# The compression's weight parts in one matmul of 512 columns, and its input chunk turned by VectorE and DMA

## The chip, the cores and the metric

The kernel runs on one core of a Trainium2 chip. The metric is the device time of one execution in microseconds; a run of the program is compared with runs of the other version on the same chip. Engine names are those of the profile: PE is TensorE (PEld its weight loads), DVE is VectorE, ACT is ScalarE, POOL is GpSimd, SP is the engine that issues most DMAs.

## What is computed

One layer of a hybrid decoder block on a sequence of 256 tokens and a width of 2048, in fp32. What matters for this change, cut from the reference:

```python
hn = rms_norm(h, ln_gain[l])
z = split_columns(hn @ w_in[l] + b_in[l])
y_a = rglru_branch(z['lru_x'], ...) * silu(z['lru_gate'])
k_c = rms_norm(compress(z['nsa_k_cmp'], cmp_pos[l, 0], cmp_w1[l, 0], cmp_w2[l, 0]), ...)
v_c = compress(z['nsa_v_cmp'], cmp_pos[l, 1], cmp_w1[l, 1], cmp_w2[l, 1])
y_b = nsa_branch(q_b, k_c, v_c, ...) * silu(z['nsa_gate'])
...
merged = mg[0] * (y_a @ w_branch[0]) + mg[1] * (y_b @ w_branch[1]) + mg[2] * (y_c @ w_branch[2])
h = h + merged @ w_out[l]
...
def compress(t, pos, w1, w2):        # blocks of 32 tokens, one each 16 tokens: 15 of them
    flat = blocks + pos               # 15 x 4096 for each of two heads
    return silu(flat @ w1) @ w2       # w1: 4096 x 256
```

The input projection `hn @ w_in` and the products behind it are almost all the arithmetic. The compression `flat @ w1` is a product with only 30 rows (15 blocks, two heads) for the keys and 30 for the values.

## The kernel before, in words

**The weight stream.** PE works through one long list of weight pieces, called halves (lines 76 to 155 make the list). A half is 128 partitions by 1024 columns, 512 KB, and arrives by one DMA into a `raw` tile, of which there are six. Each half is cut in two parts by `cut` (line 418): `wh`, the rounded copy that ACT makes, and `wl`, the rest, which DVE makes by subtracting `wh` from `raw`. Both kinds of tile have four buffers (line 422), so the conversion of a half may start only when PE is through with the half four places before. `by_rows` (line 440) then multiplies with three matmuls of 512 columns each, high by `wh`, high by `wl`, low by `wh`, for two k tiles and two row tiles: 12 matmuls a half, into the banks named `main`.

**Side work.** Everything else (turning results, the recurrence, attention, softmax) is written as small tasks whose steps are put between the matmuls of the stream. `Side.tick` (line 257) runs a task's next step when a clock of estimated costs, kept while the program is written out, allows it. A step that needs another engine's result calls `settle` and is held until the clock of PE stands a margin beyond the estimated end of that result; a step behind a DMA calls `landed`. So an added or removed instruction moves the place of all side work behind it, until the work catches up. Once written out, the order on each engine is fixed, and each engine works strictly in it.

**The compression.** The chunk of columns that feeds it (both `nsa_k_cmp` and `nsa_v_cmp`, 512 columns by 256 tokens) is turned by `turn_cmp` (line 719): ACT copies two PSUM banks of 128x512 to tiles `z`, PE transposes eight blocks of 128x128 into two PSUM banks, and ACT copies these with the bias into `k_zc`, four copies of 128x256. Then DVE lays the 15 overlapping blocks out as `k_xf` (128x960, once for keys, once for values), and a split gives `k_xs`: 60 columns for each of 32 positions, 30 of the high part and 30 of the low. 16 of the halves hold `w1`. For such a half the main loop (lines 1338 to 1350) runs, for four k tiles, a matmul of 256 columns with `wh` and another with `wl`, both with the same 60 columns of `k_xs` as the weights that stay in the array, and into one bank (`cmpb`), keys in its left 256 columns and values in its right. `cmp_end` (line 829) copies the whole bank to `hs`, 60x512, and goes on from there.

**What else stands near.** `turn_chunk` (line 704) turns the other chunks without PE: ACT copies both banks to a `k_zt` tile, DVE transposes it in 32x32 blocks (one instruction, 128x1024), four DMAs of 128 KB on SP's queue move the blocks to their place, and ACT applies the bias. `lru_task` (line 741), one for each fourth of the recurrence, convolves on DVE (`k_uc`), splits the result into `k_ucs`, splits its gate weights into `k_wds`, and has eight matmuls of 256 columns with them. `kk_task` (line 902) normalises the attention keys: squares and scales on ACT, POOL and DVE (`k_zn`), a transpose, four DMAs that move the blocks, and copies into `kk` on ACT. `y_split` (line 1091) multiplies a branch's result with its gate and splits it into `k_yh` and `k_yl` in four parts, one for each half of the product with `w_branch`.

Of the kernel before, what the change touches and what calls it, by code (L numbers as in the profile page):

```python
# [11 lines left out]
R32 = mybir.dt.float32r  # L12
AF = mybir.ActivationFunctionType
OP = mybir.AluOpType
AX = mybir.AxisListType

P = 128
D = 2048
S = 256
NT = S // P  # L20
# [6 lines left out]
NCMP = 15  # L27
NR = 32
HID = 256
# [296 lines left out]
def block_kernel(ctx: ExitStack, tc: tile.TileContext, io):  # L326
# [6 lines left out]
    wp = pool("wp")  # L333
# [11 lines left out]
    def nm(s):  # L345
        uid[0] += 1
        return f"{s}_{uid[0]}"
# [7 lines left out]
    def two(shape, dt=F32, name="b2"):  # L355
        return k2.tile(shape, dt, tag="k2", name=nm("k2_" + name))
# [12 lines left out]
    side = Side(range(4), MOST, clock, ROOMS)  # L369
# [48 lines left out]
    def cut(h, k=0, nk=None, late=False):  # L418
        m, n = h["nk"] * h["n"], h["n"]
        nk = nk or h["nk"]  # L420
        if k == 0:
            h["whl"] = [wp.tile([P, 1024], R32, tag=x, bufs=AHEAD + 1, name=nm(x)) for x in ("wh", "wl")]
        wh, wl = h["whl"]
        for a, b in parts_of(h, k, nk):
            if late:
                A.activation(wh[:, a:b], h["raw"][:, a:b], AF.Copy)
                due.append((wl[:, a:b], h["raw"][:, a:b], f(wh[:, a:b])))
            else:
                split(wh[:, a:b], wl[:, a:b], h["raw"][:, a:b])
        h["wh"] = wh[:, :m].rearrange("p (k n) -> p k n", n=h["n"])  # L430
        h["wl"] = wl[:, :m].rearrange("p (k n) -> p k n", n=h["n"])
# [48 lines left out]
    st = {}  # L480
# [181 lines left out]
    def blocks(x):  # L662

        return x.rearrange("p (n a j) -> p n a j", a=4, j=32)
# [39 lines left out]
    def turn_chunk(read, out, into, dst, k0, name):  # L704

        yield from side.wait("rs")
        yield from side.room(k4=1)
        x = mid([P, 4 * S], name="zt")
        for t, z in enumerate(celled(x)):
            A.activation(z, cells(out[t]), AF.Copy, scale=rsr[:, t:t + 1])  # L710
        side.done.add(read)
        yield from cross(x, x, flat(dst[:, k0:k0 + 4, :]).rearrange("p (b n j) -> p b n j", b=4, j=32))
        yield from side.wait("vec")
        for q in range(0, 4, 2):
            into(dst, k0 + q, moved(x)[:, 2 * q:2 * q + 4], name)
            yield True
        side.give(k4=1)

    def turn_cmp(read, out, into, dst, k0, name):

        yield from side.wait("rs")
        z = [two([P, 512], name="z") for _ in range(NT)]
        for t in range(NT):
            A.activation(z[t], out[t], AF.Copy, scale=rsr[:, t:t + 1])
            yield True
        side.done.add(read)
        yield from side.settle()
        yield from side.wait("vec")
        for q in range(2):
            b, = yield from side.take()  # L730
            for c in range(2):
                for t in range(NT):
                    T.transpose(banks[b][:, c * S + t * P:c * S + (t + 1) * P],
                                z[t][:, (2 * q + c) * P:(2 * q + c + 1) * P], ident)
            yield True
            into(dst, k0 + 2 * q, blocks(banks[b]), name)
            side.back(b)
            yield True


    def lru_task(i):
        yield from side.wait("vec", f"lru_x{i // 2}")
# [67 lines left out]
    def cmp_task(out):  # L810

        z = mid([P, 4, S], name="zc")
        yield from turn_cmp("cmpz", out, biased_cols, z, 0, "cmp")
        st["xs"] = []
        for kv in range(2):
            x = mid([P, NR, 2 * NCMP], name="xf")
            src = z[:, 2 * kv:2 * kv + 2, :]
            win = bass.AP(tensor=src.tensor, offset=src.offset,
                          ap=[list(src.ap[0]), [1, NR], [S, 2], [16, NCMP]])
            pos = vec[:, VEC["pos"] + NR * kv:VEC["pos"] + NR * (kv + 1)]  # L820
            V.tensor_tensor(x.rearrange("p r (g i) -> p r g i", g=2), win,
                            pos[:, :, None, None].to_broadcast([P, NR, 2, NCMP]), op=OP.add)
            yield True
            xs = big([P, NR, 4 * NCMP], R32, name="xs")
            split(xs[:, :, :2 * NCMP], xs[:, :, 2 * NCMP:], x)
            st["xs"].append(xs)
            yield True

    def cmp_end():
        b = st["cmpb"]  # L830
        w2 = two([P, 2, 2, P], name="w2")
        G.dma_start(w2, io["w2"])
        hs = two([4 * NCMP, 512], name="hs")
        A.activation(hs, banks[b][:4 * NCMP, :], AF.Copy)
        yield from side.settle()

        for q in range(4):
            T.transpose(banks[b][:, q * 4 * NCMP:(q + 1) * 4 * NCMP], hs[:, q * P:(q + 1) * P],
                        ident[:4 * NCMP, :4 * NCMP])
        yield True  # L840
        hz = banks[b][:, :4 * 4 * NCMP].rearrange("p (q s i) -> p q s i", q=4, s=2)
        hp, hid, sg = (one([P, 4, 30], name="hid") for _ in range(3))
        A.activation(hp, hz[:, :, 0], AF.Copy)
        V.tensor_tensor(hp, hz[:, :, 1], hp, op=OP.add)
        A.activation(sg, hp, AF.Tanh, scale=0.5)
        V.tensor_scalar(sg, sg, 1.0, 0.5, op0=OP.add, op1=OP.mult)
        V.tensor_tensor(hid, hp, sg, op=OP.mult)

        hid2 = one([P, 2, 2, 2, 16], name="hid2")
        G.memset(hid2, 0.0)  # L850
        for i in range(2):
            V.tensor_copy(hid2[:, :, :, i, :NCMP], hid[:, 2:, :].rearrange("p q (g i) -> p q g i", g=2))
        yield from side.settle()
        for q in range(2):
            T.matmul(banks[b][:30, 128:256], hid[:, q, :], w2[:, 0, q, :], start=q == 0, stop=q == 1)
        for q in range(2):
            T.matmul(banks[b][:64, 256:256 + P], hid2[:, q].rearrange("p g c i -> p (g c i)"), w2[:, 1, q, :],
                     start=q == 0, stop=q == 1)
        yield True
        for g in range(2):  # L860
            v = banks[b][32 * g:32 * g + 32, 256:256 + P]
            for i in (g, 2 + g):
                A.activation(vc4[32 * i:32 * i + 32, g, :], v, AF.Copy)
            for i in (1 - g, 3 - g):
                V.tensor_tensor(vc4[32 * i:32 * i + 32, g, :], v, f(vc4[32 * g:32 * g + 32, g, :]), op=OP.subtract)
        yield True
        ss, kc = sml([P, 1], name="kcs"), one([P, P], name="kc")
        A.activation(kc[:30, :], banks[b][:30, 128:256], AF.Square, accum_out=ss[:30, :])
        rsqrt(ss[:30, :], ss[:30, :], HD)
        yield from side.powers()  # L870
        V.tensor_scalar(kc[:30, :], banks[b][:30, 128:256], ss[:30, :], None, op0=OP.mult)
        yield from side.settle()
        T.transpose(banks[b][:, :30], kc[:30, :], ident[:30, :30])
        yield True
        src = banks[b][:, :30].rearrange("p (g i) -> p g i", g=2)
        yield from side.wait("kk")
        split(st["kh"][:, :, 256:256 + NCMP], st["kl"][:, :, 256:256 + NCMP], src, gqn)
        side.back(b)
        yield True
# [419 lines left out]
    for i, h in enumerate(halves):  # L1299
# [28 lines left out]
        if kind == "ple":  # L1328
            out = by_rows(h, lambda k: (pTh[:, k, :], pTl[:, k, :]))
        elif kind in ("rows", "turned"):  # L1330
            out = by_rows(h, halves_of(hn))
        elif kind == "proj":
            out = by_rows(h, lambda k: (st["ys"][0][:, k, :], st["ys"][1][:, k, :]))
        elif kind == "out":
            out = by_rows(h, halves_of(st["mt"]))
        elif kind == "gate":
            out = by_rows(h, halves_of(st["ht"]))
        else:
            kv = h["key"]
            if h["first"] and kv == 0:  # L1340
                st["cmpb"] = side.free.pop(0)[0]
            for k in range(h["nk"]):
                if 2 * k == h["nk"]:
                    low_parts()
                for q, w in enumerate((h["wh"], h["wl"])):
                    T.matmul(banks[st["cmpb"]][:4 * NCMP, kv * HID:(kv + 1) * HID], st["xs"][kv][:, h["k"] + k, :],
                             w[:, k, :], start=h["first"] and k == 0 and q == 0 and kv == 0,
                             stop=h["last"] and k == h["nk"] - 1 and q == 1 and kv == 1)
            if h["last"] and kv == 1:
                side.urge("cmpend", cmp_end())  # L1350
        if h["last"]:
# [117 lines left out]
```

## Time and profile before

| | us |
|---|---|
| median of three runs (lowest, highest) | 1061.61 (1061.18, 1062.3) |
| the profiled execution, its own time | 1063.0 |
| its span, first to last instruction | 1061.2 |
| PE busy in the span | 1053.4 (99%) |
| DVE busy | 768.1 (72%) |
| ACT busy | 620.7 (58%) |

Where a row of the profile begins with two numbers they are the start and the length in us, from the start of the span. A bracket behind it is the idle time of that engine just before, with what ended it. In rows that group instructions the numbers behind the bar are the busy time of all and the mean of one in ns. All instructions are recorded by one helper, so all have the line L208; they are told apart by their tiles. Matmuls overlap, so what one costs is read from the distance between starts, not from its length.

### The profile page before, as it was taken

Reading aid. Unit: us, or ns where it says so; the run is one execution under the profiler, and the core shown is the slowest. Engines: PE = TensorE matmul, PEld = TensorE weight load, DVE = VectorE, ACT = ScalarE, POOL = GpSimd, SP = SyncE. Lnnn points to the kernel's source line nnn. Section 1 sums busy time; section 2 is a strip of 40 time slices with the busy share of each in tenths; the row PEclk is TensorE's granted clock in tenths of the full one; section 3 lists DMA queues with packets and bytes.
Section 4 is the critical chain, followed back from the end, with each engine's and each line's share of the span. In section 5 each row is a group of like instructions: output and inputs, shape, how many; then the busy total and the mean of one; then the engine's idle time right before and its main releaser. Section 6 shows DMA issues by size and latency. Waiting matters only on the chain.

```text
span 1061.2 us, 14096 instructions
## 1 busy us (share of the span) xinstructions
PE 1053.4 (99%) x4927; PEld 880.5 (83%) x4927; DVE 768.1 (72%) x1135; ACT 620.7 (58%) x940; POOL 51.3 (5%) x77
## 2 busy tenths in 40 slices
PE   9999999999999999999999999999999999999998
PEld 7888898888888888888888888888888888888886
DVE  6777888897796877668878865565766566666664
ACT  7668976867767757445646544455555444444442
POOL 0000000110000000010110000000001000000000
PEclk9999999999999999999999999999999999999999
DMA  9767867787666666568677566776676876788761
GB/s 335 262 200 250 262 204 254 241 268 228 199 211 208 188 198 206 173 225 249 196 225 237 192 222 202 225 213 213 217 242 199 262 240 217 237 250 254 280 210 60
DMA packets 86295, 237.52 MB, mean 224 GB/s; under 512 B 14024, under 2 KB 31312, under 8 KB 86224
## 3 DMA queue, kind: packets, MB, share of 16 engines
q1 hardware_dynamic: 81504, 220.87, 64.6%
q0 software_dynamic: 4720, 15.76, 5.5%
q8 instruction: 38, 0.62, 0.2%
q14 instruction: 33, 0.27, 0.1%
HBM read 215.61 MB, written 4.20 MB: 207 GB/s over the span
## 4 chain that ended last, share of the span: by engine, by line
PE 97%; DMA 1%; DVE 1%; ACT 0%; SPq 0%; issue 0%; ACTq 0%; DVEq 0%
PE main L208 92%; PE bank L208 5%; DMA k_zn<-k_zt 1%; DVE wl L208 0%; DMA raw<-in_w 0%; SPq L208 0%; ACT wh L208 0%; DVE k_zn L208 0%; DVE k_fin L208 0%; ACT kk L208 0%; DVE k_ucs L208 0%; DVE sp_nss L208 0%; ACT k_fin L208 0%; ACTq L208 0%; DVEq L208 0%
## 5 line engine op out<-in xcount | busy, mean ns | idle before, releaser
L208 ACT ACTIVATE wh<-raw 128x1024 fp32r<-128x1024 f32 (+2 forms) x388 | 401.5, 1042 | 326.8 <-PE main L208 288.6
L208 DVE TENSOR_TENSOR wl<-raw,wh 128x1024 fp32r<-128x1024 f32 (+2 forms) x388 | 460.1, 1197 | 182.2 <-ACT wh L208 181.7
L208 PE MATMUL main<-wh,k_hnh 128*128 128x512 f32 (+2 forms) x1026 | 394.7, 385 | 1.2 <-ACT wh L208 1.2
L208 PE MATMUL main<-wl,k_hnh 128*128 128x512 f32 (+2 forms) x1026 | 392.7, 383 | 1.0 <-DVE wl L208 1.0
L208 PE MATMUL main<-wh,k_hnl 128*128 128x512 f32 (+1 forms) x1024 | 392.2, 383 | 0.0
L208 PEld LDWEIGHTS main<-wh,k_hnh 128*128 128x128 f32 x1026 | 192.9, 188 | 38.6 <-ACT wh L208 2.3
L208 PEld LDWEIGHTS main<-wl,k_hnh 128*128 128x128 f32 x1026 | 192.9, 188 | 37.3 <-DVE wl L208 1.6
L208 PEld LDWEIGHTS main<-wh,k_hnl 128*128 128x128 f32 x1024 | 192.1, 188 | 37.7
L208 PE MATMUL main<-wh,k_yh 128*128 128x512 f32 x192 | 75.0, 391 | 0.0
L208 PE MATMUL main<-wh,k_yl 128*128 128x512 f32 x192 | 74.8, 389 | 0.0
L208 PE MATMUL main<-wl,k_yh 128*128 128x512 f32 x192 | 74.8, 389 | 0.0
L208 PE MATMUL main<-wh,k_mth 128*128 128x512 f32 x128 | 49.8, 389 | 0.0
L208 PE MATMUL main<-wl,k_mth 128*128 128x512 f32 x128 | 49.8, 389 | 0.0
L208 PE MATMUL main<-wh,k_mtl 128*128 128x512 f32 x128 | 49.8, 389 | 0.0
L208 PE MATMUL main<-wh,k_hth 128*128 128x512 f32 x128 | 49.8, 389 | 0.0
L208 PE MATMUL main<-wl,k_hth 128*128 128x512 f32 x128 | 49.8, 389 | 0.0
L208 PE MATMUL main<-wh,k_htl 128*128 128x512 f32 x128 | 49.8, 389 | 0.0
L208 PEld LDWEIGHTS main<-wh,k_yl 128*128 128x128 f32 x192 | 36.0, 188 | 7.5
L208 PEld LDWEIGHTS main<-wh,k_yh 128*128 128x128 f32 x192 | 36.1, 188 | 7.4
L208 PEld LDWEIGHTS main<-wl,k_yh 128*128 128x128 f32 x192 | 36.1, 188 | 7.2
L208 ACT ACTIVATE k_mg<-k_mg 128x512 f32<-128x512 f32 x24 | 15.2, 634 | 28.5 <-DVE k_mg L208 28.3
L208 PEld LDWEIGHTS main<-wh,k_mth 128*128 128x128 f32 x128 | 24.0, 188 | 5.0
(243 smaller groups left out, 952.7 us busy)
## 6 DMA issues: line engine op xcount, KB each, us to landing
raw<-in_w SPq DMA_DIRECT2D x369, 512.0 KB, 4.5
bias<-in_b_in POOLq DMA_DIRECT2D x21, 256.0 KB, 5.2
raw<-in_w SPq DMA_DIRECT2D x8, 408.0 KB, 3.8
k_pz<-k_prob SPq DMA_DIRECT2D x16, 128.0 KB, 4.3
e_dram<-k_e POOLq DMA_DIRECT2D x4, 512.0 KB, 3.6
k_merged<-k_zt SPq DMA_DIRECT2D x16, 128.0 KB, 3.3
k_xc<-in_x POOLq DMA_DIRECT2D x4, 512.0 KB, 6.3
k_hx<-k_zt SPq DMA_DIRECT2D x16, 128.0 KB, 3.7
```

Of the source, the lines that this page charges most:

```text
L208: r = call(out, *args, **kw)
```

## The change

The compression's two matmuls for a k tile become one of 512 columns: `wh` and `wl` are now the two halves of one tile `whl` (same four buffers), and the moving operand takes 256 columns of each. The bank then holds the products with `wh` and `wl` side by side, for the keys alone or the values alone. When the keys are through, ACT copies the left part to `hs`, DVE adds the right part, and the values start in the bank anew; the same is done when they are through, so the copy in `cmp_end` goes. `turn_cmp` goes too, and the chunk is turned by `turn_chunk`.

```diff
-            h["whl"] = [wp.tile([P, 1024], R32, tag=x, bufs=AHEAD + 1, name=nm(x)) for x in ("wh", "wl")]
-        wh, wl = h["whl"]
+            h["whl"] = wp.tile([P, 2, 1024], R32, tag="whl", bufs=AHEAD + 1, name=nm("whl"))
+        wh, wl = h["whl"][:, 0], h["whl"][:, 1]
...
-    def turn_cmp(read, out, into, dst, k0, name):
-        z = [two([P, 512], name="z") for _ in range(NT)]
-        for t in range(NT):
-            A.activation(z[t], out[t], AF.Copy, scale=rsr[:, t:t + 1])
-            yield True
...
-                    T.transpose(banks[b][:, c * S + t * P:c * S + (t + 1) * P],
-                                z[t][:, (2 * q + c) * P:(2 * q + c + 1) * P], ident)
-            yield True
-            into(dst, k0 + 2 * q, blocks(banks[b]), name)
...
-        yield from turn_cmp("cmpz", out, biased_cols, z, 0, "cmp")
+        yield from turn_chunk("cmpz", out, biased_cols, z, 0, "cmp")
...
-        hs = two([4 * NCMP, 512], name="hs")
-        A.activation(hs, banks[b][:4 * NCMP, :], AF.Copy)
+        hs = st["hs"]
...
                 st["cmpb"] = side.free.pop(0)[0]
+                st["hs"] = two([4 * NCMP, 512], name="hs")
+            hz = banks[st["cmpb"]][:4 * NCMP, :].rearrange("p (s n) -> p s n", s=2)
             for k in range(h["nk"]):
                 if 2 * k == h["nk"]:
                     low_parts()
-                for q, w in enumerate((h["wh"], h["wl"])):
-                    T.matmul(banks[st["cmpb"]][:4 * NCMP, kv * HID:(kv + 1) * HID], st["xs"][kv][:, h["k"] + k, :],
-                             w[:, k, :], start=h["first"] and k == 0 and q == 0 and kv == 0,
-                             stop=h["last"] and k == h["nk"] - 1 and q == 1 and kv == 1)
+                T.matmul(hz, st["xs"][kv][:, h["k"] + k, :], h["whl"][:, :, k * HID:(k + 1) * HID],
+                         start=h["first"] and k == 0, stop=h["last"] and k == h["nk"] - 1)
+            if h["last"]:
+                part = st["hs"][:, kv * HID:(kv + 1) * HID]
+                A.activation(part, hz[:, 0], AF.Copy)
+                V.tensor_tensor(part, part, hz[:, 1], op=OP.add)
```

The side work moves with it. The first place is PE just behind the first `w1` half. `bank<-…,k_xs` are the compression's matmuls, those with `k_ucs` and `k_wds` the first fourth of the recurrence. In the program before, the halves there are `wh_743` (the first one of `w1`), `wh_765` and `wh_787`, and the recurrence stands in the middle of the last of them:

```order
L208 MATMUL main_83<-wh_787,k_hnh_128 128x512
L208 MATMUL main_83<-wl_788,k_hnh_128 128x512
L208 MATMUL main_83<-wh_787,k_hnl_129 128x512
L208 MATMUL bank_87<-k_ucs_711,k_wds_811 128x256 x4
L208 MATMUL bank_88<-k_ucs_712,k_wds_811 128x256 x4
L208 MATMUL main_84<-wh_787,k_hnh_128 128x512
```

After, `whl_717` is the first half of `w1`:

```order
L208 MATMUL main_84<-whl_696,k_hnl_129 128x512
L208 MATMUL bank_88<-whl_717,k_xs_650 60x512 x4
L208 MATMUL bank_89<-k_ucs_662,k_wds_751 128x256 x4
L208 MATMUL bank_90<-k_ucs_663,k_wds_751 128x256 x4
L208 MATMUL main_83<-whl_742,k_hnh_128 128x512 x2
```

The eight matmuls of the recurrence have moved one and a half halves (18 matmuls of the stream) towards the start, right behind the first `w1` half, and all of the stream stands behind them.


The second place is DVE on the way there, up to the split of the gate weights (`k_wds`, whose low part these rows make). Before:

```order
L208 TENSOR_TENSOR wl_744<-raw_647,wh_743 128x1024
L208 STREAM_TRANSPOSE k_u_566<-k_zt_759 128x1024
L208 TENSOR_TENSOR wl_766<-raw_674,wh_765 128x1024
L208 TENSOR_TENSOR k_ucs_711<-k_uc_710,k_ucs_711 64x256 x2
L208 TENSOR_TENSOR wl_788<-raw_692,wh_787 128x1024
L208 TENSOR_TENSOR k_ucs_712<-k_uc_710,k_ucs_712 64x256 x2
L208 TENSOR_TENSOR k_wds_811<-k_wd_713,k_wds_811 128x512
```

And after, where the subtractions of the weights are `whl<-raw,whl`:

```order
L208 TENSOR_TENSOR whl_696<-raw_595,whl_696 128x1024
L208 TENSOR_TENSOR k_ucs_662<-k_uc_661,k_ucs_662 64x256 x2
L208 TENSOR_TENSOR whl_717<-raw_614,whl_717 128x1024
L208 TENSOR_TENSOR k_ucs_663<-k_uc_661,k_ucs_663 64x256 x2
L208 STREAM_TRANSPOSE k_u_547<-k_zt_736 128x1024
L208 TENSOR_TENSOR whl_742<-raw_637,whl_742 128x1024
L208 TENSOR_TENSOR k_wds_751<-k_wd_664,k_wds_751 128x512
```

The split of the gate weights stood two subtractions behind that of the first `w1` half (`wl_744`); it stands one behind it (`whl_717`) now.

The third place is DVE ahead of the product of the recurrence with `w_branch`, where the parts of `k_yl` are made (two instructions a part) and `k_mg` is the merge gate's chunk, read from PE's `main` banks. Before, with the last part:

```order
L208 STREAM_TRANSPOSE k_gn_2562<-k_zt_2792 128x1024
L208 TENSOR_TENSOR wl_2784<-raw_2682,wh_2783 128x1024
L208 TENSOR_TENSOR k_yl_567<-k_yl_567,k_gl_980 128x512
L208 TENSOR_TENSOR k_yl_2702<-k_yl_567,k_yh_2701 128x512
L208 TENSOR_TENSOR wl_2806<-raw_2721,wh_2805 128x1024
```

After, with the third and the fourth part:

```order
L208 SCALAR_TENSOR_TENSOR k_mg_2779<-main_85,rsr,bias_2646 128x512
L208 SCALAR_TENSOR_TENSOR k_mg_2780<-main_86,rsr,bias_2646 128x512
L208 TENSOR_TENSOR whl_2787<-raw_2695,whl_2787 128x1024
L208 TENSOR_TENSOR whl_2804<-raw_2712,whl_2804 128x1024
L208 TENSOR_TENSOR k_yl_548<-k_yl_548,k_gl_936 128x512
L208 TENSOR_TENSOR k_yl_2681<-k_yl_548,k_yh_2680 128x512
L208 TENSOR_TENSOR k_yl_548<-k_yl_548,k_gl_936 128x512
L208 TENSOR_TENSOR k_yl_2681<-k_yl_548,k_yh_2680 128x512
```

The third and fourth part stand behind the merge chunk now; before, all four stand ahead of it. On ACT the copy that makes the third part's `k_yh` stands behind the conversion of the half `whl_2821`, which takes the buffer of the second of the four halves of that product.

More of the change, by code (lines that the diff above doesn't have):

```diff
@@ L717, in turn_chunk @@
         side.give(k4=1)
-    def turn_cmp(read, out, into, dst, k0, name):
-        yield from side.wait("rs")
-        z = [two([P, 512], name="z") for _ in range(NT)]
-        for t in range(NT):
-            A.activation(z[t], out[t], AF.Copy, scale=rsr[:, t:t + 1])
-            yield True
[L726 to L732, printed above, removed]
-                    T.transpose(banks[b][:, c * S + t * P:c * S + (t + 1) * P],
-                                z[t][:, (2 * q + c) * P:(2 * q + c + 1) * P], ident)
-            yield True
-            into(dst, k0 + 2 * q, blocks(banks[b]), name)
-            side.back(b)
-            yield True
     def lru_task(i):
```

## The prediction

> **What bounds the kernel now.** I read the page first (busy shares, the clock, the chain that ended last), then the waits of PE, then the chain's pieces in order of time.
>
> ```profile
> PE 1053.4 (99%) x4927; PEld 880.5 (83%) x4927; DVE 768.1 (72%) x1135; ACT 620.7 (58%) x940; POOL 51.3 (5%) x77
> PEclk9999999999999999999999999999999999999999
> PE 97%; DMA 1%; DVE 1%; ACT 0%; SPq 0%; issue 0%; ACTq 0%; DVEq 0%
> PE main L208 <- ACT wh L208: 1.2, 2, 0.8
> PE main L208 <- DVE wl L208: 1.0, 2, 0.8
> ```
>
> PE is the bound: 99% busy, 97% of the chain, at one clock throughout, and its waits (us in total, times, longest) come to 2.2 us. So a change can gain little beyond the PE time it removes and those 2.2 us, and it can lose wherever it makes PE wait, since no slack on PE would take that up. What PE pays for an instruction is read from the chain (start, length, count):
>
> ```profile
> 52.32 2.75 PE main L208 x12
> 55.07 0.44 PE bank L208 x4
> 55.51 23.17 PE main L208 x102
> 78.68 0.93 PE bank L208 x8
> 155.03 0.83 PE bank L208 x7
> ...
> 159.20 0.42 DVE k_ucs L208
> ...
> 159.65 0.42 DVE k_ucs L208
> ...
> 168.69 7.62 DMA k_zn<-k_zt
> ...
> 296.06 0.73 PE bank L208 x6
> 618.34 438.03 PE main L208 x1932
> ```
>
> A matmul of 512 columns costs 438.03 / 1932 = 0.2267 us, a half of twelve 2.73 (2.75 in the first row), a group of four transposes 0.44, and the eight matmuls of 256 columns of one `w1` half 0.93, or 0.117 each. The chain leaves PE for long only once, at 155.86, through ACT, DVE (a pair of `k_ucs` among it) and the moves of `k_zn` to the copies into `kk`. There PE lost its 2.2 us:
>
> ```profile
> 177.57 0.28 PE L208 MATMUL bank<-wl,k_xs 128*60 128x256 f32 x1
> 178.70 0.51 PE L208 MATMUL main<-wh,k_hnh 128*128 128x512 f32 x1 [0.84 <-ACT wh L208]
> 179.96 0.50 PE L208 MATMUL main<-wl,k_hnh 128*128 128x512 f32 x1 [0.75 <-DVE wl L208]
> 176.41 1.28 ACT L208 ACTIVATE kk<-k_zn,gqn 128x128 fp32r<-128x128 f32 x4 [3.36 <-DMA k_zn<-k_zt]
> ```
>
> ACT stood 3.36 us for the moves, and the next half's conversion stood behind it. Without a wait the two matmuls of `main` would have started at about 177.7 and 177.9; the second started at 179.96.
>
> **The change, term by term, on PE.** *Transposes.* Two groups of four go: −2 × 0.44 = **−0.88 us**, at 52 and 55 us. Nothing covers them; they are in the chain.
>
> *Wide matmuls.* Four of 512 columns take the place of eight of 256, in 16 halves:
>
> ```profile
> L208 PE MATMUL bank<-wh,k_xs 128*60 128x256 f32 x64 | 15.7, 280 | 0.0
> L208 PE MATMUL bank<-wl,k_xs 128*60 128x256 f32 x64 | 15.7, 279 | 0.0
> L208 PEld LDWEIGHTS bank<-wh,k_xs 128*60 128x60 f32 x64 | 8.4, 131 | 0.5
> ```
>
> 4 × 0.2267 = 0.907 against 0.93 to 0.94: about −0.027 a half, **−0.43 us** in all, 11 halves of it (−0.30) before 178 us. No matmul of before reads its moving columns in two pieces; bounds: at the 0.117 of a narrow one for each 256 columns nothing is gained (0), and a gain beyond −0.43 needs the loads (rival 4). I take −0.43, since the columns are as many and the groups have no other gap. The Trainium skill ("TensorE: Matmul & The Clock Gate", section "Back-to-back issue gap") gives 262 and 518 cycles at 2.4 GHz for isolated matmuls of 256 and 512 columns, 109 and 216 ns; by that the sixteen halves would gain 0.16 us by my estimate. The trace has 117 and 227 for the two, so the measured pair stands.
>
> *First new wait: the recurrence's first matmuls.* They now stand right behind the first `w1` half, which by PE's pace ends at 78.52 − 0.88 + 0.91 = 78.55 us, and the second of them needs the low part of `k_wds`. When is that there? The rows of before with the durations:
>
> ```profile
> 56.93 1.06 ACT L208 ACTIVATE wh<-raw 128x1024 fp32r<-128x1024 f32 x1 [0.55 <-PE main L208]
> 78.52 0.28 PE L208 MATMUL bank<-wh,k_xs 128*60 128x256 f32 x1
> 59.17 1.85 DVE L208 TENSOR_TENSOR k_xf<-k_zc,vec 128x960 f32<-128x960 f32 x1
> 62.11 1.16 DVE L208 TENSOR_TENSOR k_xs<-k_xf,k_xs 128x960 fp32r<-128x960 f32 x1 [1.09 <-ACT k_xs L208]
> 70.62 0.41 DVE L208 TENSOR_SCALAR k_uc<-k_u,vec 128x256 f32<-128x256 f32 x1
> 71.07 1.52 DVE L208 SCALAR_TENSOR_TENSOR k_uc<-k_u,vec,k_uc 128x255 f32<-128x255 f32 x3
> 72.50 1.22 DVE L208 TENSOR_TENSOR wl<-raw,wh 128x1024 fp32r<-128x1024 f32 x1
> 76.66 1.24 DVE L208 STREAM_TRANSPOSE k_u<-k_zt 128x1024 f32<-128x1024 f32 x1
> 79.03 0.87 DVE L208 TENSOR_TENSOR k_ucs<-k_uc,k_ucs 64x256 fp32r<-64x256 f32 x2
> 82.09 0.69 DVE L208 TENSOR_TENSOR k_wds<-k_wd,k_wds 128x512 fp32r<-128x512 f32 x1
> ```
>
> In before `k_wds` was ready at 82.78 for a start near 83.7, so it had 0.9 us to spare. In the new order DVE has ahead of it, from the subtraction of `whl_616`: six subtractions (about 1.17 from start to start), two `k_xf` (1.85), two low parts of `k_xs` (1.1), two sets of `k_uc` (72.50 − 70.62 = 1.88), two pairs of `k_ucs` (0.9), a transpose (1.16) and `k_wds` (0.69): 7.0 + 3.7 + 2.2 + 3.8 + 1.8 + 1.2 + 0.7 = 20.4 us, with 0.3 for one wait on ACT. It can't begin earlier, because the conversion of that half waits for a buffer: ACT's row at 56.93 is such a conversion, released by PE; the next one follows one half later, and 0.88 sooner by the transposes: 56.93 + 2.73 − 0.88 = 58.78, and its copy ends at 59.84. So `k_wds` is ready at 59.9 + 20.7 = 80.6 us, while PE is there at 78.67: **+1.9 us** (0 if DVE is quicker by that much, 2.5 if each step has 0.03 more). Both conversions behind it have their buffers by then, so PE loses no more.
>
> *The wait at `kk`.* ACT and SP have the `k_zn` moves at the same place as before. PE comes with −0.88 − 0.30 + 1.9 = +0.7. The chain that sets the end of this wait left PE at 155.86 and ran through DVE's queue to the moves; ahead of the moves that queue now has the addition to `hs` more (60x256; the nearest row is `k_uc`'s 0.41) and the pair of `k_ucs` (159.20 and 159.65, 0.9) less. So the end moves by +0.7 − 0.5 = +0.2 to +0.7; PE's own pace would bring it there 1.5 us or more before, so the wait stays. I take **+0.6 at 180 us**, from the upper part, as SP's moves queue behind the same weight loads. The remaining five `w1` halves: −0.13.
>
> *Second new wait: the third part of `k_yh`.*
>
> ```profile
> 298.00 0.39 PE L208 MATMUL main<-wh,k_yh 128*128 128x512 f32 x1
> 282.78 0.69 DVE L208 TENSOR_TENSOR k_yl<-k_yl,k_yh 128x512 fp32r<-128x512 f32 x1 [0.70 <-ACT k_yh L208]
> 298.20 0.75 DVE L208 SCALAR_TENSOR_TENSOR k_mg<-main,rsr,bias 128x512 f32<-128x512 f32 x1 [0.25 <-PE main L208]
> L208 ACT ACTIVATE k_yh<-k_yl x4: 633/634/634, 268.5 to 282.1; 128x512 fp32r<-128x512 f32 x4
> ```
>
> Before, all four parts were done by 283.5, 14 us ahead of their first use. Now the third stands on ACT behind the conversion of `whl_2821`, which waits until PE is through with the product's second half. From that moment T: conversion at T + 0.27 (the lag of such rows: 0.55 idle, released inside it), 1.06 long, then `k_yh` 0.63: ready at T + 1.96, and the low part 0.69 later at T + 2.65. PE has one attention group of 0.73 (row at 296.06) before the third half, so it waits 1.2 for the high part and 0.15 for the low one: **+1.4 us** (bounds: 0 if the conversion finds its buffer early, which the order excludes, to 2.7 if the fourth part is late by as much). DVE's part of it is over in time. It stands behind the second `k_mg`, which ends near 299, and two subtractions; the later of these needs a copy that waits for the product's first half, to 300.7 on before's clock, so copy to 301.9, subtraction to 303.1 and product with the gate to 303.8, while ACT comes to `k_yh` at T + 1.33, about 304.8.
>
> *Off the path.* The turned chunk now costs ACT the same two and four copies, DVE one transpose (1.24), SP four issues (priced in rival 3) and no PE. The values start the bank anew and so wait for the copy and the addition to `hs`; but on DVE the addition stands ahead of the subtraction that the values' first half needs anyway, so this costs nothing (at most the 0.41 of the addition, if that subtraction is what PE waits for).
>
> Sum: +0.6 − 0.13 + 1.4 = **+1.9 us**. The profiled execution took 1063.0, 1.4 over the median of 1061.61, so it would take 1064.9, and the median goes to **1063.5**. What a measurement of this kernel can tell from no change is about 0.2%, 2.1 us: 1059.5 to 1063.7.
>
> **Rivals.** *1. The first wait does not come* because DVE gains on my sum. Then PE is at `kk` with −1.2, its wait there stays, and −1.3 − 0.13 + 1.4 gives 1061.6. For it: each duration is start to start, with no slack for overlap with ACT; against: in the rows from 68 to 83 us DVE had no gap at all, and still finished `k_wds` only at 82.78.
>
> *2. Only the removed PE time counts*: −0.88 − 0.43 = −1.3, 1060.3; and if `kk`'s moves come earlier too, up to 2.1 more, 1058.2. Against it: the order has each of the two consumers nearer to its producer.
>
> *3. Slower: SP's queue.* Four more moves stand there just ahead of those of the first `k_u`.
>
> ```profile
> 44.23 6.28 SPq L208 DMA_DIRECT2D raw<-in_w  x3
> 52.55 2.58 SPq L208 DMA_DIRECT2D k_zt<-k_u  x4
> k_zt<-k_u SPq DMA_DIRECT2D x4, 128.0 KB, 3.8
> ```
>
> Issues of weights cost up to 2.1 each and four moves 2.58. The new moves can start at about 48.7, one weight load follows (to 53.4), and the moves of `k_u` end near 55.9: landed at 59.7 with the 3.8 of this row, at 63.5 with the 7.62 that the `k_zn` moves took. ACT's bias copies of `k_u` come at 60.7 and ahead of `whl_639`'s conversion; from that point on each us of lateness is one at `k_wds`. At 62.2 to 63.5 it is 1.5 to 2.8 more, and with the rest 1065.0 to 1066.3.
>
> ```profile
> L208 PEld LDWEIGHTS main<-wh,k_hnh 128*128 128x128 f32 x1026 | 192.9, 188 | 38.6 <-ACT wh L208 2.3
> ```
>
> *4. The loads count.* If weight loads held PE up, a wide matmul with a load of 60 columns (131 ns) could be cheaper than one of `main` with its load of 128 (188 ns), by up to 57 ns: 64 × 0.057 = 3.6 us beyond my sum, 1059.9, and about 1058.5 without one of the waits.
>
> Against it: the narrow matmuls come every 117 ns, less than their load's 131, and twice 117 is hardly over 227, so the loads lie beside the matmuls. The Trainium skill (same page, section "The mechanism" of packing) says that loads overlap matmuls in flight only when they target other rows of the array; these target the same, and by that rule 64 loads would be saved in full. This trace does not bear it out.
>
> **How the numbers follow.** My forecast 0.48, with a range of its own from 1062.3 to 1064.4, of which about 0.21 lies over 1063.7; rival 1 0.16; rival 2 0.12, half of it faster; rival 3 0.20, nearly all slower; rival 4 0.04, faster. So faster 0.10, same 0.50, slower 0.40. The range goes from 1060.0 (below it only the gains of rivals 2 and 4) to 1066.5 (the end of rival 3).
>
> **What would show it.** PE's waits of the changed kernel should name `bank<-k_ucs,k_wds`, waiting for DVE's `k_wds` for about 1.9 us near 78.6; again `main` at `kk`, near 180, of 1.5 to 2; and `main<-wh,k_yh`, waiting for ACT's `k_yh` for 1.2 near 304. The piece of four wide matmuls should be 0.91 long. I am wrong if the first or the last wait is under 0.5, if `k_u`'s moves land after 60.7, or if a wait of over 1 us stands at a place that is not named here.

## The result

| | us, median (lowest to highest) | ratio to before, 95% interval |
|---|---|---|
| before, 6 runs | 1061.88 (1060.82 to 1063.1) | |
| changed, 6 runs | 1070.19 (1067.61 to 1071.39) | 1.0077 [1.0068, 1.0087] |

The change makes the kernel 8.3 us slower, 0.77%. The forecast was 1063.5, with a range to 1066.5. The profiled execution of the changed kernel took 1070.08, with a span of 1068.3.

Its page, the first lines and the shares of the chain:

```profile
PE 1054.6 (99%) x4855; PEld 874.3 (82%) x4855; DVE 770.9 (72%) x1138; ACT 619.5 (58%) x941; POOL 52.8 (5%) x77
PE 97%; DMA 1%; DVE 1%; issue 0%; ACT 0%; SPq 0%; DVEq 0%; ACTq 0%
```

PE's waits in it (us in total, times, longest):

```profile
PE main L208 <- ACT k_yh L208: 3.1, 1, 3.1
PE main L208 <- DVE whl L208: 1.7, 3, 0.8
PE bank L208 <- DVE k_wds L208: 1.6, 1, 1.6
PE main L208 <- ACT whl L208: 1.0, 2, 0.8
```

The busy shares tell nothing: PE is at 99% as before, with 72 matmuls less and yet 1.2 us more of busy time. The waits tell more. There are two new ones, and both are those that the prediction named: the recurrence's `k_wds`, 1.6 us, and the split's `k_yh`, 3.1. Where they stand, with the wait in brackets:

```profile
80.55 1.10 PE L208 MATMUL bank<-k_ucs,k_wds 128*128 128x256 f32 x7 [1.61 <-DVE k_wds L208]
178.89 0.50 PE L208 MATMUL main<-whl,k_hnh 128*128 128x512 f32 x1 [0.17 <-ACT whl L208]
180.15 0.50 PE L208 MATMUL main<-whl,k_hnh 128*128 128x512 f32 x1 [0.76 <-DVE whl L208]
306.82 0.73 PE L208 MATMUL main<-whl,k_yh 128*128 128x512 f32 x2 [3.10 <-ACT k_yh L208]
386.74 0.50 PE L208 MATMUL main<-whl,k_yh 128*128 128x512 f32 x1 [0.77 <-DVE whl L208]
```

At `kk` (180 us) the changed kernel is 180.15 − 179.96 = 0.2 us behind. The long last piece of the chain starts at 625.18 where it started at 618.34, 6.8 behind. So the loss lies between, and the chain's pieces show where:

```profile
81.64 8.19 PE main L208 x36
89.84 0.93 PE bank L208 x4
...
305.50 0.61 DVE k_yl L208
...
306.13 0.64 ACT k_yh L208
...
306.82 17.11 PE main L208 x66
...
374.39 10.99 PE main L208 x48
...
385.46 1.24 DVE whl L208
...
625.18 438.03 PE main L208 x1932
```

A wide group of four takes 0.93, as the narrow eight did before, so a saving as small as the forecast one can't be read from one group (e5 has it over eight); the pace of `main` at the end is unchanged (438.03 for 1932). But the 66 matmuls behind the long wait took 17.11, and at 0.2267 each they take 14.96: 2.1 us are lost there, most of it without any wait. The windows (from, to, length, PE busy, granted clock, DMA share, GB/s) show why:

```profile
300.00:305.00 5.00, 3.71 (x20) 1.00 0.76 261
305.00:310.00 5.00, 3.18 (x8) 0.76 0.70 211
310.00:315.00 5.00, 5.00 (x22) 0.90 0.11 20
315.00:320.00 5.00, 5.00 (x24) 1.00 0.76 253
```

The granted clock fell behind the wait. Of the 6.8 us, 0.2 were there at `kk`, 3.1 are the wait for `k_yh`, 2.1 are lost behind it (most of that by the clock, see e4), and about 1.4 are the wait at 386 us: the chain leaves PE at 374.39 + 10.99 = 385.38 for a copy and a subtraction and is back on it at 386.74. (The bracket of 0.77 is less, because it counts from the modelled end of the matmul before.) Together that is 6.8.

### The profile page after: what moved, and what is told of

It reads as the page before. It is cut to its first block, busy times and chain, and to the rows that moved or that the text cites. A ratio compares the mean times of both kernels' runs of the same rounds, so it can differ in the third digit from the quotient of the medians.

```text
span 1068.3 us, 13970 instructions
## 1 busy us (share of the span) xinstructions
PE 1054.6 (99%) x4855; PEld 874.3 (82%) x4855; DVE 770.9 (72%) x1138; ACT 619.5 (58%) x941; POOL 52.8 (5%) x77
## 4 chain that ended last, share of the span: by engine, by line
PE 97%; DMA 1%; DVE 1%; issue 0%; ACT 0%; SPq 0%; DVEq 0%; ACTq 0%
PE main L208 92%; PE bank L208 5%; DMA k_zn<-k_zt 1%; DVE whl L208 0%; DMA raw<-in_w 0%; SPq L208 0%; ACT whl L208 0%; DVE k_fin L208 0%; ACT kk L208 0%; DVE k_ucs L208 0%; DVE k_wds L208 0%; ACT k_yh L208 0%; DVE k_yl L208 0%; DVE k_u L208 0%; ACT k_fin L208 0%
## 5 line engine op out<-in xcount | busy, mean ns | idle before, releaser
L208 PE MATMUL main<-whl,k_hnh 128*128 128x512 f32 (+2 forms) x2052 | 618.8, 384 | 2.2 <-DVE whl L208 1.0
L208 DVE TENSOR_TENSOR whl<-raw,whl 128x1024 fp32r<-128x1024 f32 (+2 forms) x388 | 460.2, 1198 | 194.5 <-ACT whl L208 192.0
L208 ACT ACTIVATE whl<-raw 128x1024 fp32r<-128x1024 f32 (+2 forms) x388 | 400.7, 1040 | 332.9 <-PE main L208 301.1
L208 PEld LDWEIGHTS main<-whl,k_hnh 128*128 128x128 f32 x2052 | 378.0, 188 | 78.3 <-ACT whl L208 2.5
L208 PE MATMUL main<-whl,k_hnl 128*128 128x512 f32 (+1 forms) x1024 | 392.2, 383 | 0.0
L208 PEld LDWEIGHTS main<-whl,k_hnl 128*128 128x128 f32 x1024 | 192.2, 188 | 37.9
L208 PE MATMUL main<-whl,k_yh 128*128 128x512 f32 x384 | 120.0, 394 | 4.0 <-ACT k_yh L208 3.1
L208 PE MATMUL main<-whl,k_hth 128*128 128x512 f32 x256 | 78.8, 389 | 0.0
L208 PE MATMUL main<-whl,k_mth 128*128 128x512 f32 x256 | 78.8, 389 | 0.0
L208 PE MATMUL main<-whl,k_yl 128*128 128x512 f32 x192 | 75.6, 394 | 0.0
```

Of the source, the lines that this page charges most:

```text
L208: r = call(out, *args, **kw)
```

## The experiments

All were timed against the kernel before on the same chip. The takes of the kernel before differ by up to 0.8 us from one set of runs to the next (1061.05 to 1061.88), so two runs of different sets are compared by their distance to it. Medians in us:

| run | what | median | before | ratio, 95% interval |
|---|---|---|---|---|
| e1 | wide matmuls alone | 1066.43 | 1061.05 | 1.0046 [1.0034, 1.0059] |
| e2 | new turning alone | 1062.86 | 1061.05 | 1.0014 [1.0005, 1.0022] |
| e3 | changed, split in one piece | 1069.54 | 1061.05 | 1.0079 [1.0065, 1.0092] |
| e4 | changed, wait filled | 1067.2 | 1061.05 | 1.0055 [1.0043, 1.0068] |
| e5 | wide, order of before | 1061.47 | 1061.22 | 1.0007 [0.9998, 1.0016] |
| e6 | narrow, order of wide | 1066.66 | 1061.22 | 1.0046 [1.0034, 1.0059] |
| e7 | both, order of e2 | 1062.74 | 1061.22 | 1.0015 [1.0006, 1.0024] |
| e8 | e7, first matmuls later | 1063.13 | 1061.22 | 1.0016 [1.0007, 1.0025] |
| e9 | e7, recurrence begun later | 1063.04 | 1061.59 | 1.0014 [1.0005, 1.0023] |
| e10 | changed, wait half filled | 1068.98 | 1061.59 | 1.0070 [1.0057, 1.0084] |
| e11 | before, late `kk` | 1060.83 | 1061.47 | 0.9992 [0.9984, 1.0001] |
| e12 | e9, late `kk` | 1060.88 | 1061.47 | 0.9997 [0.9988, 1.0006] |

**The theory** after the first result: the edits themselves are cheap, and the loss sits in the side work that they moved, above all in the late split and the clock behind it. **Rivals:** the wide matmul (its moving operand in two pieces, the joint tile, the bank begun anew) costs by itself; or the new turning loads DVE, ACT and SP's queue all along.

### e1 and e2: each part alone

e1 keeps `turn_cmp`, e2 keeps the two narrow matmuls and the copy in `cmp_end`.

```diff
-        yield from turn_chunk("cmpz", out, biased_cols, z, 0, "cmp")
+        yield from turn_cmp("cmpz", out, biased_cols, z, 0, "cmp")
```

> The wide matmuls alone, with the old way of turning (TensorE transposes). Theory: the change itself is cheap (0.43 us gained by the wide matmuls) and its loss sits in moved side work: the third part of the split of the recurrence's result came late (3.1 us of wait, then about 2.0 us at a lower clock). In this kernel three of the four parts stand ahead of the merge chunk on VectorE and only the fourth behind it, so the wait is that of the fourth, 0.5 us or so, with no loss of clock: 0 to 2 us over the kernel before, 1062 to 1064. The first lot of matmuls of the recurrence stands where it stood before: no wait near 79 us. Rival (the wide matmul or the joint tile costs by itself): about 6 us over the kernel before, 1068.

> The new way of turning alone, with the two narrow matmuls. Theory: the recurrence's first matmuls stand right behind the first w1 half and wait 1.6 us there, the wait at kk takes most of that up (0.2 us over before at 180 us), and the parts of the recurrence's result are all split ahead of the merge chunk, so no wait near 304: within 1 us of the kernel before, 1061 to 1063. Rival (the transpose, the moves and the copies load VectorE, ScalarE and SyncE's queue all along): 4 us or more over the kernel before.

e2 came out at the upper end of what the theory said. Its waits:

```profile
80.58 1.10 PE L208 MATMUL bank<-k_ucs,k_wds 128*128 128x256 f32 x7 [1.65 <-DVE k_wds L208]
...
378.64 0.39 PE L208 MATMUL main<-whl,k_yh 128*128 128x512 f32 x1
379.60 0.50 PE L208 MATMUL main<-whl,k_yh 128*128 128x512 f32 x1 [0.57 <-DVE whl L208]
```

1.65 at `k_wds` and about 0.7 at 380 us (the second matmul came 0.96 behind the first and not 0.23), less the 0.88 of the transposes: +1.5, measured +1.8. So no load all along is needed to explain it; the new turning moved the recurrence's first matmuls, and the wait at 380 us comes with it.

e1 fits neither side in size. It is 5.4 over before, near the rival's 6, but its profile shows a wait for `k_yh`, for the fourth part here and not the third, and again the lower clock behind it:

```profile
306.79 0.73 PE L208 MATMUL main<-whl,k_yh 128*128 128x512 f32 x2 [2.78 <-ACT k_yh L208]
```

```profile
305.00:310.00 5.00, 3.21 (x9) 0.79 0.79 284
310.00:315.00 5.00, 5.00 (x21) 0.87 0.28 107
```

So my 0.5 us for the fourth part was as wrong as the 1.2 for the third. Whether the wide matmul costs had still to be told from the order, and that is what e5 and e6 are for.

### e5 and e6: the edit without the order, the order without the edit

The order comes from the clock of estimated costs, so the two can be parted. In e5 the wide matmuls and the copies run, and the clock is told the old costs; every other instruction stands as in before. In e6 the narrow matmuls and the transposes run and the clock is told the new costs, and the order is that of e1.

```diff
-                T.matmul(hz, st["xs"][kv][:, h["k"] + k, :], h["whl"][:, :, k * HID:(k + 1) * HID],
-                         start=h["first"] and k == 0, stop=h["last"] and k == h["nk"] - 1)
+                nc.tensor.matmul(hz, st["xs"][kv][:, h["k"] + k, :], h["whl"][:, :, k * HID:(k + 1) * HID],
+                                 start=h["first"] and k == 0, stop=h["last"] and k == h["nk"] - 1)
+                for w in (h["wh"], h["wl"]):
+                    clock.add("pe", 256 / 2.4 + 13.4, hz[:, 0], [st["xs"][kv][:, h["k"] + k, :], w[:, k, :]])
```

> The wide matmuls alone (the old way of turning), as in the run with the wide matmuls alone, but written out with the order of the kernel before: the clock of estimated costs is told the old cost of the compression's matmuls and copies, so that every other instruction stands where it stood before. Theory (the wide matmul saves what it should, and the order is what costs): 0.4 us under the kernel before, 1060.6 when that has 1061.05; at most 0.5 us more for the two additions. Rival (the wide matmul, the joint tile or starting the bank anew costs): 1066, as the wide matmuls in their own order took.

> The reverse: the instructions of the kernel before, narrow matmuls and TensorE transposes, but the clock of estimated costs is told the new costs of the compression (226.7 ns for each k tile and not twice 120.1, and a copy and an addition for keys and values), so that all side work stands where it stands with the wide matmuls alone. Theory: the order alone costs, so it is as slow as the wide matmuls alone and 0.4 more: 1066 to 1067, with TensorE waiting 2.8 us for the last part of the split near 307 us and a lower granted clock behind it. Rival: as the kernel before, 1061.

e6 is as slow as e1 (1066.66 and 1066.43) though its instructions are those of before. Its wait, and then the windows around it:

```profile
307.72 0.80 PE L208 MATMUL main<-wh,k_yh 128*128 128x512 f32 x1 [2.77 <-ACT k_yh L208]
```

```profile
305.00:310.00 5.00, 2.28 (x5) 0.73 0.85 295
310.00:315.00 5.00, 5.00 (x22) 0.93 0.36 101
```

e5 is at 1061.47, with an interval that holds 1. This settles the larger part: in the median the wide matmuls neither cost nor gain anything that can be measured; the 5.4 us are the order's. On PE they do gain. From the first compression group to the ninth, before and then in e5, with the same instructions between:

```profile
78.52 0.28 PE L208 MATMUL bank<-wh,k_xs 128*60 128x256 f32 x1
154.86 0.28 PE L208 MATMUL bank<-wh,k_xs 128*60 128x256 f32 x1
```

```profile
78.22 1.09 PE L1348 MATMUL bank<-whl,k_xs 128*60 128x512 f32 x4
154.36 1.09 PE L1348 MATMUL bank<-whl,k_xs 128*60 128x512 f32 x4
```

These are 76.34 and 76.14 us: eight groups save 0.20, or 0.025 each, which would be 0.4 for all sixteen, as forecast, and is too little for the medians. One thing stays open: five of e5's eleven executions took 1062.81 to 1064.84, longer than any of the 27 of before beside it (up to 1062.59), and its one profile, of an execution of 1060.8, can't show what these waited for.

The trigger of the other order is small: the clock was told 226.7 ns for a k tile in place of 240.1, and a copy and an addition in two places in place of one copy, and with that the last fourth of the recurrence went 72 matmuls of the stream later (from place 982 to 1054 among the matmuls of `main`), and the split, which waits for it, with it.

### e3: the split in one piece

```diff
             side.done.add(f"{name}{i // 2}")
-            yield True
+            if name != "ysplit0":
+                yield True
```

> The whole change, but the four parts of the split of the recurrence's result written out one behind the other, all ahead of the merge chunk. Theory: the wait of 3.1 us near 304 and the 2.0 us at a lower clock behind it go, the rest stays: 5 us under the changed kernel, about 1065; if the wait near 385 us goes as well, 1064. Rival (the wait is only where a delay from elsewhere shows): under 2 us gained.

The wait near 304 went, and the kernel gained nothing: it is 8.5 us over the kernel before beside it, where the changed kernel was 8.3 over its own. The four parts one behind the other hold DVE while each waits for its copy on ACT, and a subtraction that PE needs stands behind all of them (its matmul, then the window):

```profile
294.68 0.50 PE L208 MATMUL main<-whl,k_hnh 128*128 128x512 f32 x1 [3.83 <-DVE whl L208]
```

```profile
295.00:300.00 5.00, 5.00 (x19) 0.66 0.74 244
```

The theory's number failed, and the rival's (under 2 us gained) came out, but the run can't decide between the two, since the edit itself brought another wait, of 3.8 us, with the clock falling behind that one too.

### e4 and e10: is it the idle time that lowers the clock?

13 matmuls (e4) or 6 (e10) by a block of noughts fill PE's wait; they add nought to the running sum, and the order of all else is that of the changed kernel.

```diff
+        if h["kind"] == "proj" and h["key"] == 0 and h["nth"] == 2:
+            for _ in range(13):
+                nc.tensor.matmul(out[0][:32], nought, h["wh"][:, 0, :], start=False, stop=False)
```

> The changed kernel with 13 matmuls by a block of noughts (512 columns, into 32 rows of the running sum, so that nothing is added) ahead of the third half of the recurrence's product, where TensorE waits for 3.1 us. The order of all else is the same. Theory (the idle time lowers the granted clock, and that costs 2.0 us behind it): the wait is filled with 2.95 us of matmuls, the granted clock stays at 1.00 behind it, and the kernel is 2 us faster than the changed one, about 1068. Rival (the matmuls behind the wait are slow for another reason, such as what they read): no gain, 1070, or 1073 if the matmuls come on top.

> The changed kernel with 6 matmuls by noughts in its wait near 304 us and not 13: they fill 1.4 of the 3.1 us and leave about 1.8 us of idle time. Theory: the clock falls by the length of the idle time, and the waits of 1.6 us at 80 us did not lower it, so it stays at 1.00 behind this one: 1067.2, as with 13 matmuls. Rival (any wait at this place slows what comes behind it): 1068.5 to 1070.

First e4's window and the piece of its chain behind the filled wait, then e10's matmul behind the wait, one that should come 0.45 later, and its windows:

```profile
305.00:310.00 5.00, 4.89 (x21) 1.00 0.43 167
```

```profile
305.37 15.53 PE main L208 x66
```

```profile
305.70 0.73 PE L208 MATMUL main<-whl,k_yh 128*128 128x512 f32 x2 [1.74 <-ACT k_yh L208]
...
307.77 1.05 PE L208 MATMUL main<-whl,k_yh 128*128 128x512 f32 x2
308.63 0.63 PE L208 MATMUL main<-whl,k_yl 128*128 128x512 f32 x1
```

```profile
305.00:310.00 5.00, 4.30 (x12) 0.71 0.48 188
310.00:315.00 5.00, 5.00 (x23) 0.95 0.31 83
```

With the wait filled the clock stayed at 1.00, and the 66 matmuls that took 17.11 in the changed kernel took 15.53, 1.6 less. So idle time does lower the clock, and that costs 1.6 us here. The windows of the changed kernel say the same: 0.76 and 0.90 granted over 5 us each are 2.4 + 1.0 = 3.4 us at half the clock, which is 1.7 us of work by my estimate. The rest of the 2.1 us behind the wait is lost at full clock as well.

The median of 1067.2 lies 3.0 under that of the changed kernel, but not all of this is the clock. By the distance to before the two are 2.2 apart (8.3 and 6.2), and between the two profiled executions 306.82 − 305.37 = 1.45 us were there before the 66 matmuls began: the profile of e4 has no wait near 180 us, though the order there is the same.

The second half of the theory fell: with 1.74 us of idle time left the clock fell as well (two matmuls in 308.63 − 307.77 = 0.86, 0.43 each and not 0.227), and the run took 1068.98. It does not fall in every execution. The mean granted clock of an execution tells: it was 0.996 to 0.998 in five of the changed kernel's six and 1.000 in the fastest (1067.61), 0.999 or 1.000 in all five of e4, 0.997 in three of e10's five and 0.999 in the two fastest (1067.2 and 1068.51).

### e7, e8 and e9: both parts, in better orders

e7 is the changed kernel with e5's edit. e8 holds the recurrence's first matmuls back as well, e9 the start of that task:

```diff
         yield from side.room(k2=4, k4=1)
+        if i == 0:
+            while len(st.get("xs", ())) < 2:
+                yield False
+            t = clock.t["pe"] + 4000.0
+            while clock.t["pe"] < t:
+                yield False
```

> Both parts of the change, with the order of the new turning alone (the clock of estimated costs is told the old cost of the compression). Theory: the new turning alone took 1062.86, the wide matmuls take 0.4 off: 1062.4, with the wait of 1.65 us at the recurrence's first matmuls and one near 379 us, and none near 304. Rival (the two parts hurt each other, by what they read or by VectorE's load): 1065 and over.

> As the run before it, and the first matmuls of the recurrence are held back by 3 us of estimated time, so that they stand 18 matmuls of the stream later, where they stood in the kernel before. Theory: the wait of 1.65 us at 80 us goes, and the removed time of TensorE shows, 0.88 and 0.43: 1060.8, or 1059.7 if the wait of 1.1 near 379 us goes too: faster than the kernel before (1061.05) by 0.3 to 1.3 us. Rival (VectorE's load takes it back elsewhere): no faster than the kernel before.

> Both parts of the change, with the clock of estimated costs told the old cost of the compression, and the first fourth of the recurrence begun only when the second set of the compression's columns is split and 4 us of estimated time have gone, so that VectorE does not have both in one stretch. Its first matmuls then stand 12 matmuls of the stream behind the first w1 half. Theory: VectorE's backlog is what made TensorE wait near 80 us (1.65 us when the matmuls stood early, 0.9 when they alone were held back); with the work itself moved the wait is 0.7 or less, none near 304 or 379, so 1.3 less of TensorE's work shows but for that: 1060.5 when the kernel before has 1061.1. Rival (the backlog comes back at kk or elsewhere): no faster than the kernel before.

e7 behaves as said: the two parts don't hurt each other. e8 and e9 removed what they were meant to remove and were no faster. In e8 the wait at `k_wds` became one of 0.90 at the next subtraction, since DVE had as much to do there as before, and its profile has the waits at `kk` that the one of e7 has not; e9 has none near 80 us, and lost time at `kk`:

```profile
79.87 0.50 PE L208 MATMUL main<-whl,k_hnh 128*128 128x512 f32 x1 [0.90 <-DVE whl L208]
178.84 0.49 PE L208 MATMUL main<-whl,k_hnh 128*128 128x512 f32 x1 [0.42 <-ACT whl L208]
180.10 0.50 PE L208 MATMUL main<-whl,k_hnh 128*128 128x512 f32 x1 [0.77 <-DVE whl L208]
```

```profile
179.13 0.50 PE L208 MATMUL main<-whl,k_hnh 128*128 128x512 f32 x1 [0.68 <-DVE whl L208]
```

The executions of e9 lie between 1061.52 and 1064.68, wider than those of before beside it (1060.84 to 1062.32). That pointed at `kk`, where ACT stands waiting for the moves of `k_zn`.

### e11 and e12: without the wait at `kk`

The copies and subtractions into `kk` are written out two halves later, so that two conversions go ahead of them on ACT; the order on PE doesn't change. They are collected in a list `later`, with the clock charged as before, and written out in the main loop:

```diff
+        while later and later[0][0] <= i:
+            for hi, lo, src, scale in later[0][1]:
+                nc.scalar.activation(hi, src, AF.Copy, scale=scale)
+            for hi, lo, src, scale in later.pop(0)[1]:
+                nc.vector.scalar_tensor_tensor(lo, src, scale, f(hi), op0=OP.mult, op1=OP.subtract)
```

> The kernel before, but the copies and subtractions into kk stand two conversions later on ScalarE and VectorE; the order on TensorE is the same. Theory (the wait at kk comes in some executions and not in others, by when the moves land, and the conversion behind the copies is what TensorE waits for): no wait near 180 us, the runs lie close together at the lower end of those of the kernel before, 1060.5, and 0 to 1 us under its median. Rival (the spread of the runs has another cause): same median and spread as the kernel before.

> Both parts of the change with the recurrence begun later (the run e9) and the copies into kk two conversions later as well. Theory (what the change takes off TensorE ahead of kk was given back there): the waits of 1.0 us near 180 us go, and the run is 1 to 2 us faster than that one, 1060 to 1061.5, and narrower; against the kernel before with late copies it gains up to 1.3 less its remaining waits. Rival: 1063 as that one.

Before with late `kk` takes 1060.83 (1060.28 to 1061.38, where before beside it has 1060.44 to 1062.81): 0.6 us less, with an interval that still holds 1, and half the spread, with no wait near 180 us in the profile. e12 takes 1060.88, 2.2 us less than e9. The wait at `kk` comes and goes from one execution to the next: the profiles of the changed kernel and of e4 have the same order there, and only the first waits at 180 us. The profiled execution of before (1063.0) had a large wait there. That the change's gain ahead of `kk` was given back at `kk` fits e9 and e12, but no run shows it step by step. And e12 is no faster than e11, nor, within its interval, than before. Its profile has 1.1 us of wait for a conversion, but that stands at 7 us, at the kernel's start, where the profile of the changed kernel has 0.8 and that of before 0.4, so it is not the change's; and 0.2 at a wide matmul. What became of the removed 1.3 us is not shown. No version of the two parts together that beats before was found.

## Why the prediction was wrong

**Right.** The two new waits stood where the order said, on the tiles that were named. `k_wds`: 1.9 forecast, 1.61 measured; DVE's sum of 20.4 us from `whl_616` held within 0.3. The wide matmuls: −0.43 forecast, and PE gains 0.025 a group in e5, too little for the medians. The transposes: −0.88 forecast, and e2's sum is in keeping with it; the position at `kk`: +0.2 to +0.7 forecast (+0.6 taken), +0.2 measured. The agreement at `kk` is in part luck: the wait there was to be 1.5 to 2 us and was 0.17 and 0.76, and in e4's execution of the same order it did not come at all.

**Wrong: the size of the second new wait**, the term "+1.4 us" with the bounds 0 to 2.7; it measured 3.10. The step that failed is "DVE's part of it is over in time". I let ACT's conversion of `whl_2821` come last, and counted DVE's chain from the merge chunk's end near 299. The rows of DVE in the changed kernel, then those of ACT:

```profile
297.48 0.43 DVE L208 SCALAR_TENSOR_TENSOR k_gn<-k_th,k_gn 128x256 f32<-128x256 f32 x1 [0.37 <-ACT k_gn L208]
297.82 2.35 DVE L208 TENSOR_TENSOR whl<-raw,whl 128x1024 fp32r<-128x1024 f32 x2
300.09 1.40 DVE L208 SCALAR_TENSOR_TENSOR k_mg<-main,rsr,bias 128x512 f32<-128x512 f32 x2
303.14 2.36 DVE L208 TENSOR_TENSOR whl<-raw,whl 128x1024 fp32r<-128x1024 f32 x2 [1.65 <-ACT whl L208]
305.42 0.68 DVE L208 TENSOR_TENSOR k_yl<-k_yl,k_gl 128x512 f32<-128x512 f32 x1
```

```profile
297.35 1.04 ACT L208 ACTIVATE whl<-raw 128x1024 fp32r<-128x1024 f32 x1
300.87 1.29 ACT L208 ACTIVATE k_mg<-k_mg 128x512 f32<-128x512 f32 x2 [2.47 <-DVE k_mg L208]
302.06 2.94 ACT L208 ACTIVATE whl<-raw 128x1024 fp32r<-128x1024 f32 x3
306.13 0.63 ACT L208 ACTIVATE k_yh<-k_yl 128x512 fp32r<-128x512 f32 x1 [1.14 <-DVE k_yl L208]
```

DVE was through with the two `k_mg` at 300.09 + 1.40 = 301.5, not near 299, since two subtractions stood right ahead of them, and ahead of these the products of another task (the gate `k_gn`) that wait for ACT one by one. Then the two engines waited for each other: ACT for `k_mg`, 2.47 us idle, so that its three conversions ran only from 302.06 to 305.0; DVE for one of these, 1.65 idle; and DVE's product for the third part ended at 306.1, where the forecast had 303.8. ACT stood 1.14 us for that product. Without it the wait would have been about 2.0 us by my estimate; the other 0.8 over the forecast 1.2 is ACT's own delay behind `k_mg`. Two queues that wait for each other in turn have to be followed row by row from a point that is known; I took one engine's arrival from PE's and the other's from the buffer.

**Not in it: what a wait costs behind its end.** I priced a wait at its length. Behind this one 2.1 us more were lost in the profile, 1.6 of it by the clock (e4). The Trainium skill bears on it ("TensorE: Matmul & The Clock Gate", part 1 on the clock gate and "HAM oscillation"): it says that an idle stretch of about 3.4 us brings the clock down to half. My second wait was 1.2 us long on paper, and I did not ask what its upper bound would bring. The trace agrees with half the clock (0.43 us for 0.227), but not with the length: 2.77, 2.78 and even 1.74 us did it, while 1.61 to 1.65 us at 80 us did not in any profile here.

**Not in it: the wait at 386 us** (1.4 from the chain), a wait of over 1 us at a place that was not named. It comes with the new turning (e2 and e7 have it near 380 us) and not with the wide matmuls (e1). I followed the order to the split and stopped; which instruction ahead of that subtraction is late was not followed up.

**The base.** I took the 2.2 us of waits at `kk` for a fixed part of the kernel. They belong to the profiled execution: the medians of before are 1.1 to 2.0 below its 1063.0, and with late `kk` they are gone. That would explain why the loss between medians (8.3) is larger than between the two profiled executions (7.1).

**The rivals.** None of those named is what happened. SP's queue (rival 3) was not it: ACT and DVE reached `k_wds` as summed. The loads (rival 4): e5's gain of 0.025 a group is the forecast's own term, far from the 0.23 a group that the loads would bring (4 × 0.057). The place of the loss was in the forecast, at half the size of its wait, without what the clock costs behind it, and without the wait at 386 us.

## What to carry to other kernels

Where a planner with estimated costs sets the order, an edit has two prices, its own and that of the order that comes out; part them by telling the planner the old costs. For the wide matmuls the first was nothing measurable and the second 5.4 us. An engine at 99% gains nothing from less work if the work behind it arrives at a wait that another engine's chain ends: look first for what is late next (`kk`), and check the wait in more than one execution. And ask of a wait of 1.7 us or more on TensorE what it costs behind its end: here 1.6 us.

## What the runs showed of the hardware that was not expected

Idle stretches of 1.74, 2.77, 2.78, 3.10 and 3.83 us on PE were each followed by matmuls at half the clock (granted 0.66 to 0.79 in the window of 5 us in which it fell). The windows come to 3.4 us at half the clock in every one of the five profiles (e6: 2.7 + 0.7, e3: 3.4 in one window), and the comparison with e4 puts the cost at 1.6 us. The clock can fall after the wait has ended: in e3 two matmuls from 295.25 to 295.71, behind the wait, still took 0.23 each, and two from 297.39 to 298.24 took 0.43. Waits of 1.61 to 1.65 us at another place, in six profiles, were not followed by a lower clock, and none of the 22 executions of e2 and e7, whose profiles have such a wait, shows a mean clock under 0.999. 13 matmuls by noughts in the wait held the clock at 1.00. What decides between 1.65 and 1.74 us, the length or the moment, was not tried. The clock fell in three of e10's five executions and in four of e6's five (1.000 in its fastest, 1065.17), but how long PE waited in those that were not profiled is not on record.
